# Two more projections in halves among a recurrence's steps, pooling sums as scans, and the last output tile in two pieces

## The chip, the cores and the metric

The kernel runs on one core of one Trainium2 chip. The metric is the device time of one execution in microseconds (us). Five engines work side by side, each through its own queue of instructions: TensorE (PE, whose weight loads appear as PEld), VectorE (DVE), ScalarE (ACT), GpSimd (POOL) and SyncE (SP, which starts most of the DMA transfers).

## The reference

One layer of a hybrid decoder trunk over 1024 tokens and 16 learned meta tokens (L = 1040) of width 1024, all in float32. Cut to what matters here:

```
u = rmsnorm(h);  q, f, i, g, v_pool, gate_a, gate_b = split(u @ w_in)
# recurrence, 4 heads of 128 keys and 128 values, state S:
f' = lb + (1 - lb) * sigmoid(f);   k = (1 - lb) * sigmoid(-f)
S[t] = f'[t] * S[t-1] + k[t] i[t]^T;   o[t] = q[t] S[t]
a = rmsnorm(o) * gain * sigmoid(g)
# pooling, 4 groups of 128 channels, windows w = 2, 4, 8, 16:
p = ((mean of the last min(w, t+1) rows of v_pool) - v_pool) @ pool_proj * scale
z = sigmoid(gate_a) * (a @ w_branch_hgrn) + sigmoid(gate_b) * (p @ w_branch_pool)
h = h + rmsnorm(z @ w_out)
u = rmsnorm(h);  y = gelu(causal_conv3(u @ w_gate) + bias) * (u @ w_up)
out = h + rmsnorm(y @ w_down)
```

## The kernel before

Nearly every matmul operand is kept as a high and a low part (`whi`/`wlo`, `uhi`/`ulo`, in a type with fewer mantissa bits that the PE takes faster), and a product is three matmuls: high by high, high by low, low by high. With the feature dimension on the partitions, a row of a projection is one matmul of 128 x 342 to 348 columns; 8 blocks of keys times 3 chunks of columns times 3 products make 72 rows for one projection.

The program runs in stages: norms, the gates `gate_a` and `gate_b` and the value projection of the recurrence (to about 265 us of the span), then **the heads' stage** (about 265 to 480 us), then the output projection and the feed-forward layer, whose products go through Strassen's scheme of seven products (to about 1090 us), and last the projection by `w_down`, whose end is the second place of the change.

**The heads' stage** is written by a table of words, `ORDER`. A word with a capital letter is a projection of one block of 128 output columns: `F`, `Q`, `G` (forget logit, query and output gate of the recurrence), `PV` (input of the pooling), `PP`, `BB`, `BA` (the products behind them), followed by the number of the head or group. `F3` is a whole projection; `Fa3` and `Fb3` are its two halves in time: `proj_parts` stops after half of its key blocks (rows L206, L207 and L210 of the profile) and goes on when the second word comes. The weights of each projection are cast on ACT (L152) and their low part taken on DVE, three blocks ahead, when the loader moves on. Between them, `h0` to `h3` take the next step of a head's recurrence (`head_steps`, a generator, one instance for each head):

- The score matrix of a head is put together from blocks on six levels (block lengths 2, 4, 8, 16, 32, 64). For each, DVE subtracts (L683), ACT takes two exponentials (L685, L686), DVE makes two products (L687, L688), all into a tile `d`, and PE multiplies it with itself into a bank `sl` (L698 for the levels from 32 up, L704 for the smaller). Levels go in pairs; a step issues DVE's and ACT's part of a pair ahead of PE's.
- Then come `kd`, the keys weighted by the decay to their chunk's end (L740 to L745), transposed on PE (L761 and L764) and copied (L762, L766); the products of the diagonal blocks (`sb`, L772); the chunk states `st` (L782 to L792, banks `ds`); the output `o` (L802 to L813, banks `po`); and the sums of its squares over the partitions (`ms`, L818 and L819), with a logarithm on ACT from each bank (L820) and one exponential (L821).

`c1` is the chain from a forget logit to its logarithm and running sum (`chain_f`, L629 to L636); ACT makes the sigmoids from the banks ahead of it (L624, L625). `sp0` and `sa0` split a pooled group or a head's output into high and low part, and `w0` to `w5` prepare weights of the feed-forward layer.

ACT changes its function table between sigmoids, exponentials, and the logarithms (an ACT_TABLE_LOAD row in the profile, at the line that needs it).

**Order.** Outside of blocks marked `manual_schedule`, the engines' orders are not those of the source: the framework's scheduler puts instructions into each engine's queue by a simulated timeline, with the order written as its start. Inside such a block the named engines follow the source. In both cases the resulting queues are fixed when the program is built, and an engine works through its own strictly in order. The tables of words thus set the order only in the large. Tiles of `slot` come from one pool of equal slots and `bank` is one of 8 PSUM banks, both handed on in turn; whoever takes one waits for the last reader of what was in it.

**Pooling.** `post_pv` copies the projection from its three banks to `vp` (ACT, L847) and forms the window sum by doubling on POOL (L854): one addition for w = 2, two for 4, three for 8, four for 16, ten in all, `cur[t] + cur[t - step]`. `pool_split` takes w times the mean minus the value on DVE.

**The end.** The last quarter of the `w_down` product, four tiles of 128 tokens by 512 columns, is summed in four banks `pd` over 22 key blocks: first the blocks from KT = 6 on for all four tiles, then the six that were prepared early (`held`), tile by tile. Behind each tile DVE subtracts (L1777), `half_norm` takes the sum of squares on ACT (L1701) and multiplies by the gain on DVE (L1702), and `finish` takes the root (ACT, L1708), its reciprocal (L1710), adds the residual for both halves of the row and stores them:

```
    for t in range(NT):
        for j in range(KT):
            multiply(banks, held[j], False, j == KT - 1, [t])
        dve.tensor_tensor(c11[t], banks[t], c11[t], ALU.subtract)
        half_norm(c11[t], t, 0)
        finish(t, c11[t], c12[t])
```

The functions that the change touches:

Of the kernel before, what the change touches and what calls it, by code (L numbers as in the profile page):

```python
# [42 lines left out]
KT = 6  # L43
# [11 lines left out]
ZA = 4  # L55
AHEAD = 3

ORDER = ("F0 c0 Q0 h0 F1 h0 h0 c1 Q1 h0 h1 h0 F2 h1 h1 c2 h0 h0 Qa2 Qb2 h1 h1 h2 G2 h0 h0 h1 Fa3 h1 h2 h0 h2 Fb3 "
# [3 lines left out]
POOLED = ()  # L62
# [7 lines left out]
def trunk_kernel(ctx: ExitStack, tc: tile.TileContext, x, meta_tokens, mix_norm_pre,  # L70
# [4 lines left out]
    act, dve, pool_e, pe = nc.scalar, nc.vector, nc.gpsimd, nc.tensor  # L75
# [43 lines left out]
    def small(shape, name, tag, bufs=4):  # L119
        return sm.tile(shape, F32, tag=tag, name=nm(name), bufs=bufs)  # L120
# [45 lines left out]
    class Loader:  # L166
# [10 lines left out]
        def next(self):  # L177
            self.at += 1
            return self.got[self.at - 1]
# [4 lines left out]
    def mm3(ps, a, b, first, last):  # L184
        (ahi, alo), (bhi, blo) = a, b
        pe.matmul(ps, ahi, bhi, start=first, stop=False)  # L186
        pe.matmul(ps, ahi, blo, start=False, stop=False)  # L187
        pe.matmul(ps, alo, bhi, start=False, stop=last)  # L188

    def proj(*a, **k):  # L190
        for banks in proj_parts(*a, **k):
            pass
        return banks
# [22 lines left out]
    class Strassen:  # L216
# [624 lines left out]

    def post_pv(g, pv):
        w = POOL_WINDOWS[g]
        vp, s1 = slot(L, name="vp"), slot(L, name="s1")
        s2 = slot(L, name="s2") if w > 2 else None
        for (lo, n), ps in zip(CH_ALL, pv):
            act.copy(vp[:, lo : lo + n], ps[:, :n])  # L847
        cur, step = vp, 1
        bufs = [s1, s2]
        while step < w:  # L850
            nxt = bufs[0]
            bufs = bufs[::-1]
            a = 2 * step - 1
            pool_e.tensor_tensor(nxt[:, a:L], cur[:, a:L], cur[:, a - step : L - step], ALU.add)  # L854
            cur, step = nxt, 2 * step
        pooled[g] = (cur, vp)

    def pool_split(g):
        w = POOL_WINDOWS[g]
        cur, vp = pooled[g]  # L860
        if w > T0 + 1:

            c1 = small([P, 1], "c1", "c1", 2)
# [128 lines left out]

    order = ORDER.split()
    order = [(o_[:-1], int(o_[-1])) for o_ in order]
# [57 lines left out]
    E = mybir.EngineType  # L1052
    with tc.manual_schedule(engines={E.Activation, E.DVE, E.PE}):
# [34 lines left out]
        for i in range(2, len(vtiles)):  # L1088
            ps = bank("pv")
# [80 lines left out]
    for kind, i in order:  # L1170
# [30 lines left out]
        if part == "a":  # L1201
# [3 lines left out]
        banks = proj(None, 0, n_k, xs, chunks, ws=ws, name="p" + kind.lower(),  # L1205
                     by_bank=2 if (kind, i) == ("BA", KD - 1) else 0)
# [307 lines left out]
    def next_rot():  # L1514
        rot[0] += 1
        return rot[0] % 2
# [138 lines left out]
    g4 = gain_bc(ffn_norm_post, "g4")  # L1655
    ssq4 = const.tile([P, 2, NCH], F32, name="ssq4")
    NT = NCH // 2

    def acc(i):
        return [big[0][:, 2 * i + t // 2, (t % 2) * 512 : (t % 2) * 512 + 512] for t in range(NT)]  # L1660

    u2, c21, c12, c11 = (acc(i) for i in range(4))
    c22 = u2

    def multiply(banks, ops, first, last, tiles=range(NT)):
        (yh, yl), (wh, wl) = ops
        for t in tiles:
            tt = slice(t * P, (t + 1) * P)
            mm3(banks[t], (yh[:, tt], yl[:, tt]), (wh, wl), first, last)

    def prep_last(k, hold):

        load_ops(3, k)
        if hold:
            hi, lo = slot(1024, F32R, "yh"), slot(1024, F32R, "yl")
        else:
            i = next_rot()
            hi, lo = big[1][:, i, :], big[1][:, 2 + i, :]
# [14 lines left out]
    junk = slot(512, name="junk4")  # L1693

    def load_h(t):
        hrow[t] = slot(D, name="hrow")
        nc.sync.dma_start(hrow[t], hs[HALO + t * P : HALO + (t + 1) * P, :])

    def half_norm(src, t, j):

        act.activation(junk, src, AF.Square, accum_out=ssq4[:, j, t : t + 1])  # L1701
        dve.tensor_tensor(src, src, g4[:, j * 512 : (j + 1) * 512], ALU.mult)  # L1702
        if j == 1:
            dve.tensor_scalar(ssq4[:, 1, t : t + 1], ssq4[:, 1, t : t + 1], 1.0 / D, EPS, ALU.mult, ALU.add)
# [27 lines left out]
    with tc.manual_schedule(engines={E.Activation, E.DVE}):  # L1732
        for s_ in range(3):
            banks = [[bank("pd") for _ in range(NT)] for _ in range(2)]
            for k in range(KH):
# [3 lines left out]
                if k == KH - 1:  # L1739
                    pa, pb = banks  # L1740
# [16 lines left out]


    banks = [bank("pd") for _ in range(NT)]
    for n, k in enumerate(range(KT, KH)):  # L1760
        if n == 0:
            prep_last(KH - 2, False)
            for t in range(NT):
                dve.tensor_tensor(c12[t], c12[t], pb[t], ALU.add)
            prep_last(KH - 1, False)
        multiply(banks, held.pop(k), n == 0, False)
        if n < NT:
            half_norm(c22[n], NT + n, 1)
            half_norm(c21[n], NT + n, 0)
            finish(NT + n, c21[n], c22[n])  # L1770
            load_h(n)
        if n > 0:
            half_norm(c12[n - 1], n - 1, 1)
    for t in range(NT):
        for j in range(KT):
            multiply(banks, held[j], False, j == KT - 1, [t])
        dve.tensor_tensor(c11[t], banks[t], c11[t], ALU.subtract)  # L1777
        half_norm(c11[t], t, 0)
        finish(t, c11[t], c12[t])
    close_pool("ps", "sm", "fm")  # L1780


# [27 lines left out]
```

## The time and the profile before

| | |
|---|---|
| time, median of 3 runs | 1324.69 us (1324.55 to 1325.63) |
| profiled execution | 1326.72 us, span 1325.0 us, mean granted PE clock 0.994 |
| PE | 1302.5 us busy, 98% of the span, 8665 matmuls |
| PEld | 1158.7 us, 87% |
| DVE | 948.7 us, 72% |
| ACT | 581.0 us, 44% |
| POOL | 355.5 us, 27% |
| heads' stage, 265 to 480 us | PE busy 204.0 of 215.0 us, DVE 153.6, ACT 145.1, POOL 24.1; granted clock 0.97 |

Shares of busy time are means over stages. The last row, from a table of busy time by stretches of the span, is for the stage that the change touches most: 11 us of PE's idle time lie in it. In the profile a row names the engine, the line, the operation, the tile written and those read, and in brackets what ended the engine's idle time ahead of it. A wait "PE sl L704 <- ACT ..." means that PE's row at L704 writing `sl` stood idle until that instruction was done.

### The profile page before, as it was taken

To read this page: it belongs to the slowest core of one execution; us is meant where nothing else is said; L and a number is where in the kernel's file an instruction comes from. 1 tells how busy PE (TensorE), PEld (TensorE's weight loads), DVE (VectorE), ACT (ScalarE), POOL (GpSimd) and SP (SyncE) were. 2 spreads that over 40 slices of the span, in tenths; PEclk is the share of its full clock that TensorE was granted. 3 is DMA by queue.
4 is the path that set the end of the run, shared out by engine and by line. 5 is a ranking of instruction groups with operands and counts; after the bars stand their busy time and mean duration, and the time that the engine had idled before them with its cause. 6 is when DMAs were issued, how large, how long until landed. Compare 5 with 4: busy or idle time off the path is not lost.

```text
span 1325.0 us, 21836 instructions
## 1 busy us (share of the span) xinstructions
PE 1302.5 (98%) x8665; PEld 1158.7 (87%) x8665; DVE 948.7 (72%) x1251; ACT 581.0 (44%) x978; POOL 355.5 (27%) x291
## 2 busy tenths in 40 slices
PE   8999999999899899999999999999999999999997
PEld 7799899999899899987898888888888888888886
DVE  6765545378768567775678999888998885455757
ACT  5553333368656755235564322222223233444443
POOL 3015422000011400061025555645646652000000
PEclk9999999999899999999999999999999999999999
DMA  8145433411110157987686777677767699666644
GB/s 273 42 107 160 125 106 103 127 50 49 36 52 20 46 180 263 353 284 253 234 281 234 179 212 191 187 206 176 175 162 168 150 258 305 212 223 222 222 175 159
DMA packets 139831, 230.55 MB, mean 174 GB/s; under 512 B 9080, under 2 KB 77340, under 8 KB 139730
## 3 DMA queue, kind: packets, MB, share of 16 engines
q1 hardware_dynamic: 127666, 204.78, 46.4%
q0 software_dynamic: 12064, 24.38, 11.2%
q8 instruction: 68, 1.11, 0.3%
q14 instruction: 33, 0.27, 0.1%
HBM read 165.59 MB, written 86.57 MB: 190 GB/s over the span
## 4 chain that ended last, share of the span: by engine, by line
PE 92%; DMA 3%; ACT 2%; DVE 1%; issue 1%; SPq 0%; DVEq 0%; ACTq 0%
PE P L309 15%; PE P L310 15%; PE P L312 15%; PE pd L186 5%; PE pd L187 5%; PE pd L188 5%; PE pm L186 2%; PE pm L187 2%; PE pm L188 2%; PE pf L206 1%; PE ppv L206 1%; PE pf L207 1%; PE ppv L210 1%; PE ppv L207 1%; PE pg L206 1%; PE pq L210 1%
## 5 line engine op out<-in xcount | busy, mean ns | idle before, releaser
L310 PE MATMUL P<-v,whi 128*128 128x512 f32 (+2 forms) x408 | 140.7, 353 | 0.0
L309 PE MATMUL P<-v,whi 128*128 128x512 f32 (+2 forms) x408 | 140.7, 352 | 0.0
L312 PE MATMUL P<-v,wlo 128*128 128x512 f32 (+2 forms) x424 | 135.1, 349 | 0.0
L1544 DVE TENSOR_TENSOR rot<-wraw,rot 128x1024 fp32r<-128x1024 f32 x31 | 38.0, 1224 | 72.2 <-ACT rot L1543 72.2
L309 PEld LDWEIGHTS P<-v,whi 128*128 128x128 f32 x408 | 76.7, 188 | 10.4
L310 PEld LDWEIGHTS P<-v,whi 128*128 128x128 f32 x408 | 76.6, 188 | 10.2
L254 ACT CAST whi<-wraw 128x512 fp32r<-128x512 f32 x78 | 46.1, 618 | 86.7 <-PE P L310 63.1
L312 PEld LDWEIGHTS P<-v,wlo 128*128 128x128 f32 x424 | 74.0, 188 | 10.8
L188 PE MATMUL pd<-rot 128*128 128x512 f32 x272 | 82.1, 389 | 0.0
L187 PE MATMUL pd<-rot 128*128 128x512 f32 x272 | 82.1, 389 | 0.0
L186 PE MATMUL pd<-rot 128*128 128x512 f32 x272 | 81.1, 389 | 0.1
L280 POOL TENSOR_TENSOR swa<-wraw,wraw 128x512 f32<-128x512 f32 x28 | 44.8, 1601 | 133.2 <-DMA wraw<-in_ffn_w_gate_dram 68.1
L1543 ACT CAST rot<-wraw 128x1024 fp32r<-128x1024 f32 x31 | 32.7, 1054 | 90.7 <-PE pd L188 89.4
L254 ACT CAST whi<-swa 128x512 fp32r<-128x512 f32 x56 | 33.4, 618 | 81.8 <-PE P L310 74.4
L255 DVE TENSOR_TENSOR wlo<-wraw,whi 128x512 fp32r<-128x512 f32 x74 | 65.6, 908 | 2.7 <-ACT whi L254 2.7
L255 DVE TENSOR_TENSOR wlo<-swb,whi 128x512 fp32r<-128x512 f32 x56 | 62.9, 1129 | 6.5 <-ACT whi L254 6.5
L1472 DVE SCALAR_TENSOR_TENSOR y<-g,par,y 128x1024 f32<-128x1024 f32 x44 | 64.3, 1461 | 0.8
L254 ACT CAST whi<-swb 128x512 fp32r<-128x512 f32 x56 | 33.4, 618 | 70.9 <-PE P L310 66.5
L186 PEld LDWEIGHTS pd<-rot 128*128 128x128 f32 x272 | 51.1, 188 | 11.1 <-DVE p L1480 0.5
L187 PEld LDWEIGHTS pd<-rot 128*128 128x128 f32 x272 | 51.0, 188 | 10.6
L188 PEld LDWEIGHTS pd<-rot 128*128 128x128 f32 x272 | 51.0, 188 | 10.6
L309 PE MATMUL P<-t4h,whi 128*128 128x258 f32 (+1 forms) x196 | 57.0, 307 | 0.0
(414 smaller groups left out, 4000.1 us busy)
## 6 DMA issues: line engine op xcount, KB each, us to landing
wraw<-in_w_in_dram SPq DMA_DIRECT2D x36, 512.0 KB, 4.9
yt<-ysum SPq DMA_DIRECT2D x33, 512.0 KB, 5.3
wraw<-in_ffn_w_gate_dram SPq DMA_DIRECT2D x26, 512.0 KB, 7.0
wraw<-in_ffn_w_up_dram SPq DMA_DIRECT2D x22, 512.0 KB, 4.6
wsum<-in_ffn_w_down_dram SPq DMA_DIRECT2D x22, 512.0 KB, 8.2
wraw<-in_w_out_dram SPq DMA_DIRECT2D x18, 512.0 KB, 4.3
ysum<-ys SPq DMA_DIRECT2D x11, 768.0 KB, 5.9
sa<-sscr SPq DMA_DIRECT2D x16, 513.0 KB, 6.5
```

The source lines that it names most:

```text
L186: pe.matmul(ps, ahi, bhi, start=first, stop=False)
L187: pe.matmul(ps, ahi, blo, start=False, stop=False)
L188: pe.matmul(ps, alo, bhi, start=False, stop=last)
L206: pe.matmul(ps[:, :n], whi[:, k, :], xhi, start=(k == 0), stop=False)
L254: act.copy(hi, src)
L255: (pool_e if 4 <= i < 2 * self.early else dve).tensor_tensor(lo, src, rr(hi), ALU.subtract)
L280: pool_e.tensor_tensor(s1, a21, a22, ALU.add)
L309: pe.matmul(d, whi[:, k, :], xh[:, c : c + w], start=(k == 0 and onto is None), stop=False, **go)
L310: pe.matmul(d, whi[:, k, :], xl[:, c : c + w], start=False, stop=False, **go)
L312: pe.matmul(x[:, o : o + w], wlo[:, k, :], xh[:, c : c + w], start=False, stop=(k == 3), **go)
L1472: dve.scalar_tensor_tensor(a, g[:, j : j + SEQ], cvw[:, j, m : m + 1], a, ALU.mult, ALU.add)
L1544: dve.tensor_tensor(lo, src, rr(hi), ALU.subtract)
```

## The change

**In the table of words:** `G2` is cut into `Ga2 h0 Gb2`, so that one more step of head 0 comes between its halves; a step of head 0 and one of head 2 that stood ahead of `Fb3` now follow it; and `PV1`, which stood whole behind the steps `h3 h2 h3 h1`, is cut in two, its first half ahead of those steps and its second half ahead of the `h1`. **In the pooling:** the doubling additions on POOL become one scan on DVE (new value in, value of w rows before out), or one addition for w = 2; 16 zeros ahead of `vp`, set by POOL, stand for what lies ahead of row 0; and the mean of row T0 = 14 for w = 16 is a scaled window sum instead of a sum of its own. **At the end:** the last tile is summed in two pieces of 256 columns in two banks (a fifth bank `pd`), and each is subtracted, squared and multiplied by the gain by itself, the gain product into a slot of its own (`left`); ACT and DVE follow the written order there; and of the additions into `c12`, the first goes ahead of the preparation of key block KH - 2.

```diff
-... Qa2 Qb2 h1 h1 h2 G2 h0 h0 h1 Fa3 h1 h2 h0 h2 Fb3 h2 c3 h2 PVa0 ...
+... Qa2 Qb2 h1 h1 h2 Ga2 h0 Gb2 h1 Fa3 h0 h1 h2 Fb3 h0 h2 h2 c3 h2 PVa0 ...
-... Q3 h1 h3 h0 h1 h2 h3 h2 h3 h1 PV1 h3 sp0 ...
+... Q3 h1 h3 h0 h1 h2 PVa1 h3 h2 h3 PVb1 h1 h3 sp0 ...
     def post_pv(g, pv):
         w = POOL_WINDOWS[g]
-        vp, s1 = slot(L, name="vp"), slot(L, name="s1")
-        s2 = slot(L, name="s2") if w > 2 else None
+        vz, cur = slot(NM + L, name="vp"), slot(L, name="s1")
+        vp = vz[:, NM:]
+        pool_e.memset(vz[:, :NM], 0.0)
         for (lo, n), ps in zip(CH_ALL, pv):
             act.copy(vp[:, lo : lo + n], ps[:, :n])
-        ...
-            pool_e.tensor_tensor(nxt[:, a:L], cur[:, a:L], cur[:, a - step : L - step], ALU.add)
-            cur, step = nxt, 2 * step
+        if w == 2:
+            dve.tensor_tensor(cur, vp, vz[:, NM - 1 : NM - 1 + L], ALU.add)
+        else:
+            dve.tensor_tensor_scan(cur, vp, vz[:, NM - w : NM - w + L], 0.0, ALU.add, ALU.subtract)
     def pool_split(g):
-            dve.tensor_reduce(c1, vp[:, 0 : T0 + 1], mybir.AxisListType.X, ALU.add)
-            dve.tensor_scalar(cur[:, T0 : T0 + 1], c1, float(w) / (T0 + 1), None, ALU.mult)
+            dve.tensor_scalar(cur[:, T0 : T0 + 1], cur[:, T0 : T0 + 1], float(w) / (T0 + 1), None, ALU.mult)
 ...
+    pieces = [(banks[-1], slice(0, 256)), (bank("pd"), slice(256, 512))]
+    def multiply_pieces(ops, first, last, which=pieces):
+        ...
+            mm3(ps[:, :256], (yh[:, tt], yl[:, tt]), (wh[:, n], wl[:, n]), first, last)
         if n == 0:
+            dve.tensor_tensor(c12[0], c12[0], pb[0], ALU.add)
             prep_last(KH - 2, False)
-            for t in range(NT):
+            for t in range(1, NT):
                 dve.tensor_tensor(c12[t], c12[t], pb[t], ALU.add)
-        multiply(banks, held.pop(k), n == 0, False)
+        ops = held.pop(k)
+        multiply(banks, ops, n == 0, False, range(NT - 1))
+        multiply_pieces(ops, n == 0, False)
 ...
+    with tc.manual_schedule(engines={E.Activation, E.DVE}):
+        for t in range(NT):
+            left = lefts[t % 2]
+            for i, (ps, n) in enumerate(pieces if t == NT - 1 else ((banks[t], slice(0, 512)),)):
+                ...
+                dve.tensor_tensor(c11[t][:, n], ps[:, : n.stop - n.start], c11[t][:, n], ALU.subtract)
+                part = t == NT - 1 and i == 0
+                act.activation(junk[:, n], c11[t][:, n], AF.Square, accum_out=sums4 if part else ssq4[:, 0, t : t + 1])
+                dve.tensor_tensor(left[:, n], c11[t][:, n], g4[:, n], ALU.mult)
+                if part:
+                    dve.scalar_tensor_tensor(ssq4[:, 1, t : t + 1], sums4, 1.0 / D, ssq4[:, 1, t : t + 1],
+                                             ALU.mult, ALU.add)
+            finish(t, left, c12[t])
```

Three places show what this does to the engines' queues. The number behind a name is the number of its buffer, which is not the same before and after. **Place A** is ACT's queue at the end of projection F3. Before, `d_3867` and `d_3873` are head 2's levels 8 and 16, `whi_3917` is the cast of the next weights, and `pf_3711` to `pf_3713` are the banks of F3:

```order
L783 COPY st_3813<-ds_3814 128x128
L685 ACTIVATE d_3867<-d_3867 128x64x8
L686 ACTIVATE d_3867<-d_3867 128x64x8
L685 ACTIVATE d_3873<-d_3873 128x32x16
L686 ACTIVATE d_3873<-d_3873 128x32x16
L152 CAST whi_3917<-wraw_3915 128x1024
L624 ACT_TABLE_LOAD
L624 ACTIVATE f_3923<-pf_3711 128x348
L625 ACTIVATE kk_3921<-pf_3711 128x348
```

In the same place after the change the same two levels are `d_3919` and `d_3925`, and F3's banks are `pf_3673` to `pf_3675`:

```order
L152 CAST whi_3851<-wraw_3849 128x1024
L624 ACT_TABLE_LOAD
L624 ACTIVATE f_3857<-pf_3673 128x348
L625 ACTIVATE kk_3855<-pf_3673 128x348
L624 ACTIVATE f_3857<-pf_3674 128x346
L625 ACTIVATE kk_3855<-pf_3674 128x346
L624 ACTIVATE f_3857<-pf_3675 128x346
L625 ACTIVATE kk_3855<-pf_3675 128x346
L783 COPY st_3865<-ds_3866 128x128
L685 ACT_TABLE_LOAD
L685 ACTIVATE d_3919<-d_3919 128x64x8
L686 ACTIVATE d_3919<-d_3919 128x64x8
```

The copy and the exponentials have moved from ahead of the cast to behind F3's sigmoids, with a table load ahead of them.

**Place B** is ACT's queue at head 1's sums of squares, where `d_4472` and `d_4478` are head 3's levels 8 and 16, `ms_4484` to `ms_4492` head 1's sums, and `vp_4580` takes PV1. Before:

```order
L685 ACTIVATE d_4472<-d_4472 128x64x8
L686 ACTIVATE d_4472<-d_4472 128x64x8
L820 ACT_TABLE_LOAD
L820 ACTIVATE rs_4325<-ms_4484,eps_t 128x342
L820 ACTIVATE rs_4325<-ms_4488,eps_t 128x342
L820 ACTIVATE rs_4325<-ms_4492,eps_t 128x342
L685 ACT_TABLE_LOAD
L685 ACTIVATE d_4478<-d_4478 128x32x16
L686 ACTIVATE d_4478<-d_4478 128x32x16
L821 ACTIVATE rs_4325<-rs_4325 128x1026
L152 CAST whi_4576<-wraw_4574 128x1024
L847 COPY vp_4580<-ppv_4499 128x348
```

After it, the levels are `d_4512` and `d_4518`, the sums `ms_4573` to `ms_4581`, and PV1 goes to `vp_4566`:

```order
L152 CAST whi_4562<-wraw_4560 128x1024
L820 ACT_TABLE_LOAD
L820 ACTIVATE rs_4326<-ms_4573,eps_t 128x342
L685 ACT_TABLE_LOAD
L685 ACTIVATE d_4512<-d_4512 128x64x8
L686 ACTIVATE d_4512<-d_4512 128x64x8
L820 ACT_TABLE_LOAD
L820 ACTIVATE rs_4326<-ms_4577,eps_t 128x342
L848 COPY vp_4566<-ppv_4376 128x348
L848 COPY vp_4566<-ppv_4377 128x346
L848 COPY vp_4566<-ppv_4378 128x346
L820 ACTIVATE rs_4326<-ms_4581,eps_t 128x342
```

The cast and the copies of `vp` come earlier, level 8's exponentials stand between the first and the second logarithm instead of ahead of them, and two more changes of table stand in the row (the fourth, ahead of `d_4518`, is the row behind the last one shown).

On PE the same place reads, before (`ppv_4499` to `ppv_4501` are the banks of PV1):

```order
L210 MATMUL ppv_4499<-uhi_88,wlo_3918 128x348
L210 MATMUL ppv_4500<-uhi_88,wlo_3918 128x346
L210 MATMUL ppv_4501<-uhi_88,wlo_3918 128x346
L704 MATMUL sl_4588<-d_4472 32x16 x32
L704 MATMUL sl_4627<-d_4478 32x16 x32
L206 MATMUL ppv_4677<-uhi_88,whi_4151 128x348
```

and after (`ppv_4376` to `ppv_4378` are the banks of PV1):

```order
L210 MATMUL ppv_4378<-uhi_88,wlo_3852 128x346
L818 MATMUL ms_4573<-rh_4353,onesr 128x342
L819 MATMUL ms_4573<-rl_4354,onesr 128x342
L818 MATMUL ms_4577<-rh_4353,onesr 128x342
L819 MATMUL ms_4577<-rl_4354,onesr 128x342
L818 MATMUL ms_4581<-rh_4353,onesr 128x342
L819 MATMUL ms_4581<-rl_4354,onesr 128x342
L704 MATMUL sl_4588<-d_4512 32x16 x32
L704 MATMUL sl_4627<-d_4518 32x16 x32
```

Head 1's `ms` sums, which stood ahead of most of PV1, have moved behind it, directly ahead of the two level products.

More of the change, by code (lines that the diff above doesn't have):

```diff
@@ L56 @@
 AHEAD = 3
-ORDER = ("F0 c0 Q0 h0 F1 h0 h0 c1 Q1 h0 h1 h0 F2 h1 h1 c2 h0 h0 Qa2 Qb2 h1 h1 h2 G2 h0 h0 h1 Fa3 h1 h2 h0 h2 Fb3 "
[1 row of a table removed]
+ORDER = ("F0 c0 Q0 h0 F1 h0 h0 c1 Q1 h0 h1 h0 F2 h1 h1 c2 h0 h0 Qa2 Qb2 h1 h1 h2 Ga2 h0 Gb2 h1 Fa3 h0 h1 h2 Fb3 "
[1 row of a table added]
          "sp1 PVb3 h2 h3 h3 sp3 PP1 h0 G3 h3 w0 PP2 PP3 w1 BB0 w4 h2 w4 BB1 BB2 BB4 w5 h3 BB3 w4 h3 w5 sa2 BB5 w5 "
@@ L843, in post_pv @@
         w = POOL_WINDOWS[g]
-        vp, s1 = slot(L, name="vp"), slot(L, name="s1")
-        s2 = slot(L, name="s2") if w > 2 else None
+        vz, cur = slot(NM + L, name="vp"), slot(L, name="s1")
+        vp = vz[:, NM:]
+        pool_e.memset(vz[:, :NM], 0.0)
         for (lo, n), ps in zip(CH_ALL, pv):
             act.copy(vp[:, lo : lo + n], ps[:, :n])
[L848 to L853, printed above, removed]
-            pool_e.tensor_tensor(nxt[:, a:L], cur[:, a:L], cur[:, a - step : L - step], ALU.add)
-            cur, step = nxt, 2 * step
+        if w == 2:
+            dve.tensor_tensor(cur, vp, vz[:, NM - 1 : NM - 1 + L], ALU.add)
+        else:
+            dve.tensor_tensor_scan(cur, vp, vz[:, NM - w : NM - w + L], 0.0, ALU.add, ALU.subtract)
         pooled[g] = (cur, vp)
@@ L861, in pool_split @@
         if w > T0 + 1:
-            c1 = small([P, 1], "c1", "c1", 2)
-            dve.tensor_reduce(c1, vp[:, 0 : T0 + 1], mybir.AxisListType.X, ALU.add)
-            dve.tensor_scalar(cur[:, T0 : T0 + 1], c1, float(w) / (T0 + 1), None, ALU.mult)
+            dve.tensor_scalar(cur[:, T0 : T0 + 1], cur[:, T0 : T0 + 1], float(w) / (T0 + 1), None, ALU.mult)
         dve.scalar_tensor_tensor(cur[:, T0:L], cur[:, T0:L], 1.0 / w, vp[:, T0:L], ALU.mult, ALU.subtract)
@@ L1759, in trunk_kernel @@
     banks = [bank("pd") for _ in range(NT)]
+    pieces = [(banks[-1], slice(0, 256)), (bank("pd"), slice(256, 512))]
+    def multiply_pieces(ops, first, last, which=pieces):
+        (yh, yl), (wh, wl) = ops
+        tt = slice((NT - 1) * P, NT * P)
+        for ps, n in which:
+            mm3(ps[:, :256], (yh[:, tt], yl[:, tt]), (wh[:, n], wl[:, n]), first, last)
     for n, k in enumerate(range(KT, KH)):
         if n == 0:
+            dve.tensor_tensor(c12[0], c12[0], pb[0], ALU.add)
             prep_last(KH - 2, False)
-            for t in range(NT):
+            for t in range(1, NT):
                 dve.tensor_tensor(c12[t], c12[t], pb[t], ALU.add)
             prep_last(KH - 1, False)
-        multiply(banks, held.pop(k), n == 0, False)
+        ops = held.pop(k)
+        multiply(banks, ops, n == 0, False, range(NT - 1))
+        multiply_pieces(ops, n == 0, False)
         if n < NT:
@@ L1773, in trunk_kernel @@
             half_norm(c12[n - 1], n - 1, 1)
[L1774 to L1779, printed above, removed]
+    lefts = [slot(512, name="left") for _ in range(2)]
+    sums4 = small([P, 1], "sums4", "mq", 6)
+    with tc.manual_schedule(engines={E.Activation, E.DVE}):
+        for t in range(NT):
+            left = lefts[t % 2]
+            for i, (ps, n) in enumerate(pieces if t == NT - 1 else ((banks[t], slice(0, 512)),)):
+                for j in range(KT):
+                    if t == NT - 1:
+                        multiply_pieces(held[j], False, j == KT - 1, pieces[i : i + 1])
+                    else:
+                        multiply(banks, held[j], False, j == KT - 1, [t])
+                dve.tensor_tensor(c11[t][:, n], ps[:, : n.stop - n.start], c11[t][:, n], ALU.subtract)
[6 more added lines that the diff above has]
+            finish(t, left, c12[t])
     close_pool("ps", "sm", "fm")
```

2 rows, old and new, of the table ORDER are left out of this document.

## The prediction

> **What bounds the kernel now.** I read the page's chain of waits first, then TensorE's (PE's) list of waits, then PE's busy time and clock in short windows.
>
> ```profile
> PE 92%; DMA 3%; ACT 2%; DVE 1%; issue 1%; SPq 0%; DVEq 0%; ACTq 0%
> PE pg L206 <- ACT rs L820: 3.4, 1, 3.4
> PE sl L704 <- issue: 2.7, 1, 2.7
> PE sb L772 <- DVE kk L754: 2.3, 1, 2.3
> PE sl L698 <- DVE near L719: 1.1, 1, 1.1
> PE ppv L206 <- ACT kk L625: 0.7, 1, 0.7
> ```
>
> PE is the bound nearly everywhere, so another engine's work costs something only where PE waits for it. The five waits below the first line lie among the heads' steps and sum to 10.2 us. Each long one is paid twice, as these windows of 3.41 us show (columns: PE busy, weight loads, DVE, ACT, POOL, granted clock, DMA share, GB/s):
>
> ```profile
> 335.02:338.44 3.42, 1.17 (x70) 0.91 (x68) 3.42 (x8) 3.37 (x7) 0.00 (x0) 1.00 0.52 152
> 338.44:341.85 3.41, 2.28 (x56) 2.08 (x43) 3.41 (x6) 3.40 (x6) 0.00 (x0) 0.50 0.02 5
> 341.85:345.27 3.42, 3.42 (x13) 3.42 (x13) 3.28 (x6) 3.35 (x8) 0.00 (x0) 0.50 0.07 19
> 399.88:403.29 3.41, 0.68 (x19) 0.64 (x19) 0.28 (x2) 2.59 (x4) 0.00 (x0) 1.00 0.03 10
> 403.29:406.71 3.42, 3.42 (x14) 3.42 (x13) 3.35 (x6) 2.18 (x3) 0.00 (x0) 0.50 0.02 5
> 457.90:461.31 3.41, 0.88 (x5) 0.88 (x6) 2.90 (x3) 3.38 (x7) 2.01 (x1) 1.00 0.00 0
> 461.31:464.73 3.42, 3.42 (x14) 3.42 (x13) 1.33 (x2) 3.39 (x5) 0.00 (x0) 0.50 0.52 156
> ```
>
> A window in which PE is busy for 0.68 to 2.28 of its 3.41 us is followed by one at half clock. PE works 2.28 + 3 x 3.42 = 12.5 us at half clock; at full clock that is about half the time, so some 6 us are lost. These stalls cost 10 + 6 = 16 us: that is the stake of the reordering, and it can be lost as well as won.
>
> **The change, part by part.** Times are those of the profiled execution: 1326.7 us with a span of 1325.0; the median of the three runs is 2.0 us lower.
>
> *G2 in halves.* Head 0's transposes of `kd` (L761) now follow G2's first half. Here are the first matmul of the second half before, and the product of `kd` for which the transposes wait:
>
> ```profile
> 328.86 0.32 PE L206 MATMUL pg<-uhi,whi 128*128 128x342 f32 x1
> 329.70 1.23 DVE L745 TENSOR_TENSOR kd<-kd,kk 128x1040 f32<-128x1040 f32 x1
> ```
>
> PE comes to the transposes at 328.86 and waits until 330.93: 2.1 us. In return the waits of 2.3 and 1.1 us go: the block product L772 now stands behind 36 more rows of G2 and half of F3, and its operand on DVE is done by then. Net -1.3 in idle time; one half-clock window in place of two.
>
> *Place A, behind F3.* Before, ACT made head 2's exponentials of levels 8 and 16 (L685, L686, buffers 3867 and 3873) before F3 ended, and 30 rows of F3 still covered DVE's products. Now the same exponentials (3919, 3925) stand on ACT behind the cast that waits for F3's end, a table load, F3's six sigmoids, a copy and another table load. The prices:
>
> ```profile
> 353.45 0.63 ACT L685 ACTIVATE d<-d 128x512 f32<-128x512 f32 x1
> 353.99 0.61 ACT L686 ACTIVATE d<-d 128x512 f32<-128x512 f32 x1
> 354.14 0.68 DVE L688 TENSOR_TENSOR d<-d,kk 128x512 f32<-128x512 f32 x1
> 358.94 1.05 ACT L152 CAST whi<-wraw 128x1024 fp32r<-128x1024 f32 x1 [4.34 <-PE pf L207]
> 360.01 1.28 ACT L624 ACT_TABLE_LOAD   x1
> 361.30 0.46 ACT L624 ACTIVATE f<-pf 128x348 f32<-128x348 f32 x1
> 363.01 0.51 ACT L625 ACTIVATE kk<-pf 128x346 f32<-128x346 f32 x1
> 387.14 0.29 ACT L783 COPY st<-ds 128x128 f32<-128x128 f32 x1
> 350.55 0.48 PE L782 MATMUL ds<-vmeta,ktm 16*128 16x128 f32 x2
> 352.54 0.41 PE L206 MATMUL pf<-uhi,whi 128*128 128x348 f32 x1
> 359.31 1.33 PE L704 MATMUL sl<-d 128*32 128x16 f32 x128
> ```
>
> From the cast's start to the last sigmoid's end: 363.52 - 358.94 = 4.58. Copy 0.29, table load 1.28, the pair of exponentials 1.15 (353.45 to 354.60), DVE's product 0.68: together 8.0 us before PE may do level 8. In that time PE has F3's last three rows (0.5), the `ds` matmuls (350.55 to 352.54: 2.0) and half of what row 359.31 shows (0.7): 3.2 us. Idle: at least 4.8. ACT may also be late at the cast: it had 4.34 us to spare, but now has two more table loads ahead (the sigmoids of G2 are cut apart by exponentials) and copies that wait for DVE, so between 0 and 2.6 late; I take 1.4, about the middle: 6.2. Level 16 waits 0.6 more (another pair of exponentials, less PE's 0.6 on level 8), and the 0.7 at `ppv` goes. The next block product, for head 1, stands behind a DVE queue set back by this: 0 up to the 2.3 of its like above; I take 0.8. Net +6.9.
>
> *Place B, PV1 in halves.* The step between the halves takes away the 2.7 us wait, since a half of PV1 stands ahead of it. But before, 48 rows of PV1 stood between head 1's `ms` sums and levels 8 and 16 of head 3; now all of PV1 is done before the sums, nothing follows, and on ACT the logarithms L820 are cut apart by the exponentials, with a table load at each change:
>
> ```profile
> 408.80 0.64 PE L819 MATMUL ms<-rl,onesr 128*128 128x342 f32 x3
> 409.53 1.42 ACT L820 ACTIVATE rs<-ms,eps_t 128x342 f32<-128x342 f32 x3
> 410.97 1.28 ACT L685 ACT_TABLE_LOAD   x1
> 377.77 1.14 ACT L847 COPY vp<-ppv 128x348 f32<-128x348 f32 x3
> ```
>
> First wait: behind PV1's last matmuls ACT has a cast 1.05, table load 1.28, one logarithm 0.5, table load 1.28, exponentials 1.15, then DVE 0.68: 6.0 us. PE has 3 rows of PV1 and 6 of `ms` at 0.16: 1.4. Idle 4.6. Second wait, counted from the end of those exponentials: table load 1.28, logarithm 0.44, three copies of `vp` 1.05, logarithm 0.44, table load 1.28, exponentials 1.15, DVE 0.68 = 6.3, against PE's 0.7 wait for the first product and 0.6 to 1.25 (half clock) on level 8: idle 4.4 to 5.0, I take 4.6. Net +9.2 - 2.7 = +6.5.
>
> *G3's wait of 3.4* goes down: its first bank is freed by a copy of the transposes (L762) instead of by L820 behind its table load. Between 0 and 3.4 remains; I take 1.6: -1.8.
>
> *Pooling on DVE.* Ten POOL additions become three scans and one addition on DVE, whose price is known from the same kind and length:
>
> ```profile
> L636 DVE TENSOR_TENSOR_SCAN b<-keep_on,f 128x1040 f32<-128x1040 f32 x4 | 9.3, 2325 | 0.2
> ```
>
> That is 3 x 2.3 + 1.2 = 8.2 us on DVE, queued ahead of head products. At A and B ACT comes last, not DVE, and POOL's sums released none of the five waits: I take 0, with 0 to 2.3 (one scan ahead of a product) for the range. The small memsets on POOL stand well ahead of their readers. SP's queue keeps its order.
>
> *The end.* The rows that carry it:
>
> ```profile
> 109.00 0.28 PE L309 MATMUL P<-uhi,whi 128*128 128x256 f32 x1
> 109.12 0.28 PE L310 MATMUL P<-ulo,whi 128*128 128x256 f32 x1
> 1317.38 0.39 PE L187 MATMUL pd<-yl,yh 128*128 128x512 f32 x1
> 1317.61 0.39 PE L188 MATMUL pd<-yh,yl 128*128 128x512 f32 x1
> 1318.04 0.69 DVE L1777 TENSOR_TENSOR acc<-pd,acc 128x512 f32<-128x512 f32 x1 [0.38 <-PE pd L188]
> 1318.76 0.63 ACT L1701 ACTIVATE junk<-acc 128x512 f32<-128x512 f32 x1 [3.03 <-DVE acc L1777]
> 1319.52 0.29 ACT L1708 ACTIVATE std<-ssq 128x1 f32<-128x1 f32 x1
> 1319.52 0.69 DVE L1702 TENSOR_TENSOR acc<-acc,g 128x512 f32<-128x512 f32 x1 [0.79 <-ACT junk L1701]
> 1320.12 0.16 DVE L1710 RECIPROCAL rstd<-std 128x1 f32<-128x1 f32 x1
> ```
>
> Half-width matmuls start 0.12 apart, full ones 0.23: 33 matmuls of the last tile become 66, +0.3 us. After the last matmul the subtraction and the square run on half the columns: they lose nearly 0.5 (the 1040-column product above took 1.23 against 0.68 for 512, so 256 take about 0.4). The gain product is off the chain, so the reciprocal follows the root: 0.25. Net -0.4. The bank that the extra piece needs is freed by the `c12[0]` addition, now first; 9 matmuls of PE cover it, and at worst PE waits that row's 0.7.
>
> **Sum.** Idle: -1.3 + 6.9 + 6.5 - 1.8 = +10.3. Half clock: 12.5 us of work before; now about one window behind the transposes, one and a half behind A, two behind and between B's waits, perhaps one behind G3: some 16 us, +1.5 (from -2 to +4). End -0.4. Together +11.4: 1326.7 + 11.4 = 1338.1 in a profiled execution, 2.0 less in the median: 1336.1.
>
> The Trainium skill, "TensorE: Matmul & The Clock Gate", Part 1, lets the clock fall to half after an idle window of about 3.4 us. The windows here fell after 0.68 to 2.28 us of work, so the trace differs; if only a fully idle window counted, some 5 us of my half-clock time would go and the sum would be about 1331.
>
> **Rivals.** (1) *Faster:* the halves feed PE where it starved, A and B hide, and all old waits go: 16 us and 0.4 won, 1308. It decides at ACT's queue: the exponentials would have to be ready before PE has done the 3.2 us at A and 1.4 us at B. For it: the two waits cut by the halves do go. Against it: 8.0 and 6.0 us of ACT and DVE rows in strict sequence. 0.04. (2) *The idle time only moves:* ACT is early at A (4.8), `vp`'s copies and logarithms hide B's second wait, head 1's product and G3 wait for nothing: 2.1 + 4.8 + 4.6 = 11.5 against 10.2, two half windows fewer, end -0.4: 1322 to 1327. Against it: B's second wait has two table loads of its own. 0.05. (3) *Every table switch costs more than its row:* ACT drains too, 1.4 us at each of six loads in A's and B's chains, 1344. Against it: 360.01 + 1.28 ends where 361.30 starts. 0.03. The Trainium skill, "ScalarE: Activation LUTs", What ACT_TABLE_LOAD costs, puts such a drain at 1.38 us beside 1.28 for the load; only the load is in the trace. (4) *The windows fall badly and a scan stands ahead of a product:* +4 and +3, 1343. 0.08. My forecast, 1329 to 1341: 0.80.
>
> **Numbers.** A measurement of this kernel tells 0.2% (2.6 us) from no change. Faster 0.05 (rival 1 and a piece of 2), same 0.05, slower 0.90. The range from 1328.5 to 1344 leaves out rivals 1 and 2 and a tail.
>
> **What would show it.** Right: PE waits at `sl` L704 for `d` L687/L688 three times, one near 6 and two of 4 to 5 us, half-clock windows behind each, 36 table loads instead of 31, no wait of 2.7 at the step inside PV1, and an end shorter by half a microsecond. Wrong: PE busy through F3's end and PV1's end; or a long wait whose releaser is a scan.

## The result and the profile after

The changed kernel takes 1333.93 us in the median (1333.54 to 1335.19, 4 runs), the kernel before 1324.62 us (1321.42 to 1325.63, 4 runs). The ratio is 1.0076, 95% interval 1.0058 to 1.0094: slower by 0.76%. The forecast was 1336.1 us, 1328.5 to 1344. The profiled execution took 1333.88 us with a span of 1332.2, that is 7.2 us more than the profiled one of before. (That one was slower than its kernel's median by 2 us, the profiled one of the changed kernel was not; so the profiles lie closer together than the medians.)

Where the 7.2 us lie is seen first in two stretches of the same work, from the first row of F0 to the first row of the first `BB` product. The first row is before, the second after (columns: PE busy, PE's weight loads, DVE, ACT, POOL, granted clock, DMA share, GB/s):

```profile
268.73:478.46 209.73, 198.73 (x2605) 191.34 (x2603) 148.42 (x212) 142.27 (x244) 24.11 (x14) 0.97 0.15 43
```
```profile
268.56:486.70 218.14, 197.53 (x2605) 189.85 (x2603) 152.10 (x215) 149.01 (x249) 3.16 (x8) 0.96 0.14 41
```

The heads' stage alone grew by 8.4 us. PE does the same 2605 matmuls and is busy for 1.2 us less, so all of it, and a little more, is idle time. PE's waits in this stage, after the change:

```profile
PE sl L704 <- DVE d L688: 16.3, 4, 5.9
PE pt L761 <- DVE kd L745: 2.0, 1, 2.0
PE pg L206 <- ACT kt L762: 1.3, 1, 1.3
```

Five waits of 10.2 us have become six of 19.6 (a wait of 0.6 to 0.7 us at `pq`, the same before and after, is left out of both). Four stand at the small levels' products, one pair at place A (the end of F3) and one at place B (head 1's sums). Here they are in the timeline of PE, with the wait ahead of each row in brackets:

```profile
361.42 1.05 PE L704 MATMUL sl<-d 128*32 128x16 f32 x64 [5.88 <-DVE d L688]
363.24 1.05 PE L704 MATMUL sl<-d 128*32 128x16 f32 x64 [0.76 <-DVE d L688]
...
421.89 1.05 PE L704 MATMUL sl<-d 128*32 128x16 f32 x64 [4.83 <-DVE d L688]
...
427.79 1.05 PE L704 MATMUL sl<-d 128*32 128x16 f32 x64 [4.85 <-DVE d L688]
```

And the sequence on ACT and DVE that PE waits for at place A, from the cast of the next weights to level 8's last product:

```profile
353.36 1.05 ACT L152 CAST whi<-wraw 128x1024 fp32r<-128x1024 f32 x1
354.43 1.28 ACT L624 ACT_TABLE_LOAD   x1
...
357.44 0.50 ACT L625 ACTIVATE kk<-pf 128x346 f32<-128x346 f32 x1
357.78 0.32 ACT L783 COPY st<-ds 128x128 f32<-128x128 f32 x1
358.12 1.28 ACT L685 ACT_TABLE_LOAD   x1
359.41 0.63 ACT L685 ACTIVATE d<-d 128x512 f32<-128x512 f32 x1
359.95 0.61 ACT L686 ACTIVATE d<-d 128x512 f32<-128x512 f32 x1
360.68 0.69 DVE L688 TENSOR_TENSOR d<-d,kk 128x512 f32<-128x512 f32 x1
```

From 353.36 to 361.37 nothing stands still on ACT and DVE together: 8.0 us, row by row what the prediction added up. The clock around the two places, in windows of 3.41 us:

```profile
356.61:360.03 3.42, 0.00 (x0) 0.00 (x0) 1.71 (x4) 3.39 (x8) 0.00 (x0) 1.00 0.52 154
360.03:363.44 3.41, 1.26 (x80) 1.15 (x84) 3.37 (x7) 3.39 (x6) 0.00 (x0) 0.50 0.00 1
363.44:366.86 3.42, 3.42 (x73) 3.38 (x66) 2.59 (x7) 2.54 (x3) 0.11 (x1) 0.50 0.02 5
418.06:421.47 3.41, 0.00 (x0) 0.00 (x0) 1.97 (x3) 3.36 (x5) 0.00 (x0) 1.00 0.07 19
421.47:424.88 3.41, 1.05 (x64) 0.95 (x64) 1.23 (x2) 3.38 (x7) 0.00 (x0) 0.50 0.02 5
424.88:428.30 3.42, 0.51 (x38) 0.54 (x42) 3.41 (x4) 3.41 (x5) 0.00 (x0) 0.50 0.00 0
428.30:431.71 3.41, 3.41 (x52) 3.37 (x45) 3.41 (x6) 0.42 (x1) 0.00 (x0) 0.50 0.00 0
```

Five windows at half clock instead of four, but in three of them PE stands idle for most of the time: 1.26 + 3.42 + 1.05 + 0.51 + 3.41 = 9.7 us of work at half clock, where it was 12.5 before. No other window of the stage is at half clock, neither behind the 2.0 at the transposes nor behind G3's 1.3.

The end: the first matmul of the last section in both kernels, then the last matmul and the reciprocal that stands on the chain to the last store, after the change (those of before are in the prediction).

```profile
1287.92 0.39 PE L186 MATMUL pd<-yh 128*128 128x512 f32 x1
```
```profile
1295.28 0.39 PE L186 MATMUL pd<-yh 128*128 128x512 f32 x1
...
1325.55 0.28 PE L188 MATMUL pd<-yh,yl 128*128 128x256 f32 x1
...
1327.28 0.16 DVE L1704 RECIPROCAL rstd<-std 128x1 f32<-128x1 f32 x1 [0.44 <-ACT std L1702]
```

From the section's first matmul to its last it is now 30.27 us, and was 29.69: +0.58. From the last matmul to the reciprocal it is 1.73, and was 2.51: -0.78.

### The profile page after: what moved, and what is told of

It reads as the page before. It is cut to its first block, busy times and chain, and to the rows that moved or that the text cites. A ratio compares the mean times of both kernels' runs of the same rounds, so it can differ in the third digit from the quotient of the medians.

```text
span 1332.2 us, 21907 instructions
## 1 busy us (share of the span) xinstructions
PE 1300.0 (98%) x8698; PEld 1158.0 (87%) x8698; DVE 956.6 (72%) x1257; ACT 588.1 (44%) x985; POOL 335.4 (25%) x285
## 4 chain that ended last, share of the span: by engine, by line
PE 92%; ACT 4%; DVE 2%; DMA 2%; issue 1%; SPq 0%; DVEq 0%; ACTq 0%
PE P L309 15%; PE P L310 15%; PE P L312 15%; PE pd L186 5%; PE pd L187 5%; PE pd L188 5%; PE pm L186 2%; PE pm L188 2%; PE pm L187 2%; PE pf L206 1%; PE pbb L206 1%; PE pbb L207 1%; PE pf L207 1%; PE pbb L210 1%; PE ppv L206 1%; PE pv L187 1%
## 5 line engine op out<-in xcount | busy, mean ns | idle before, releaser
L310 PEld LDWEIGHTS P<-v,whi 128*128 128x128 f32 x408 | 76.6, 188 | 10.2
```

The costliest lines, as they stand in the source:

```text
L310: pe.matmul(d, whi[:, k, :], xl[:, c : c + w], start=False, stop=False, **go)
```

## The experiments

The times below are ratios to the kernel before, measured on the same chip.

**e1: the end alone.** The part of the change from `banks = ...` on, with ORDER and pooling of before.

```diff
+    pieces = [(banks[-1], slice(0, 256)), (bank("pd"), slice(256, 512))]
...
+    with tc.manual_schedule(engines={E.Activation, E.DVE}):
```

> The kernel before with the change at the end alone (last tile in two pieces, the c12[0] addition first, ACT and DVE in written order); ORDER and pooling as before. My theory: -0.4 us (66 half-width matmuls cost 0.3 more than 33, and behind the last one 0.7 to 0.8 goes), so within 1 us of before; PE's waits among the heads' steps the same to 0.1 us. Rival: the written order on ACT and DVE makes the norms of the first tiles late and PE waits for the bank of the extra piece, +1 us or more.

Ratio 0.9999, interval 0.9989 to 1.0010: nothing that can be told from zero (-1.5 to +1.3 us). The times alone would not exclude the rival's microsecond, but PE has no wait in the last projection of this trace, and among the heads' steps it has the waits of before to 0.1 us.

**e2: place B alone.**

```diff
-... h2 h3 h2 h3 h1 PV1 h3 sp0 ...
+... h2 PVa1 h3 h2 h3 PVb1 h1 h3 sp0 ...
```

> The kernel before with PV1 alone in halves (place B); G2, F3, pooling and end as before. My theory: B's price is made by the order of ACT's queue, so it comes without the scans: the wait of 2.7 us at the step goes, two waits of 4.6 to 5.0 us at sl L704 for d L688 come, half-clock windows around them; +6.5 to +8 us, and G3's wait stays near 3.4 us if it hangs on the pooling, or falls to 1.3 us if it hangs on this part of the order. Rival (the scans on DVE make the loss): no wait over 3 us here and a time within 2 us of before.

Ratio 1.0069 (1.0057 to 1.0081), +9.1 us. Without any scan on DVE the two waits are there, so the order makes them; the rival falls. G3's wait stayed at 3.3 us, so this part of the order does not take it away. But the cost is above the range, and the second wait is 6.26 us where the whole change has 4.85. The timeline of this kernel at that place shows why:

```profile
419.47 1.92 POOL L854 TENSOR_TENSOR s<-s 128x1037 f32<-128x1037 f32 x1
...
419.82 2.12 DVE L687 TENSOR_TENSOR d<-d,q 128x512 f32<-128x512 f32 x1 [4.51 <-ACT d L685]
...
422.68 1.06 PE L704 MATMUL sl<-d 128*32 128x16 f32 x64 [6.26 <-DVE d L688]
```

DVE's product takes 2.12 us here, and 0.69 in the changed kernel; the difference of 1.43 is that of the two waits (1.41). A POOL addition runs beside it. Run e8 tests that.

**e3: place A and G2 alone.**

```diff
-... h2 G2 h0 h0 h1 Fa3 h1 h2 h0 h2 Fb3 h2 c3 h2 PVa0 ...
+... h2 Ga2 h0 Gb2 h1 Fa3 h0 h1 h2 Fb3 h0 h2 h2 c3 h2 PVa0 ...
```

> The kernel before with G2 in halves and the steps around F3 as in the changed kernel (place A); PV1, pooling and end as before. My theory: the waits of 2.3 and 1.1 us give way to one of 2.0 at the transposes; a wait of 5.9 and one of 0.8 us come at sl L704; the half-clock windows move from 338-345 us to those behind the 5.9; the 2.7 us wait at the step inside PV1 and G3's 3.4 us stay: +4 to +6 us. Rival (the scans make the loss): within 2 us of before. The sum of this run's and e2's difference should come to about 2 us above the whole change's, because the pooling and the end give something back.

Ratio 1.0032 (1.0021 to 1.0043), +4.2 us, inside the range. PE's waits are those expected, with 5.86 and 0.76 at place A:

```profile
PE sl L704 <- DVE d L688: 6.6, 2, 5.9
PE pg L206 <- ACT rs L820: 3.4, 1, 3.4
PE sl L704 <- issue: 2.5, 1, 2.5
PE pt L761 <- DVE kd L745: 2.0, 1, 2.0
```

G3's 3.4 is untouched here too. The two parts of the order together cost 13.3 us, about 4 more than the whole change and not the expected 2: pooling and end must give back more than I thought.

**e4: the old order with the new pooling and the new end.** The changed kernel with the table of words of before.

> The changed kernel with the table of words of before: pooling as scans on DVE and the new end, nothing else. My prediction's terms (pooling 0, end -0.4) give -0.4 us; if the fall of G3's wait (3.4 to 1.3 us) belongs to the pooling and not to the order, it appears here and the time is 2 to 4 us under before, with the half-clock window behind it gone. Rival (the 8.2 us of scans on DVE stand ahead of head products): +2 to +4 us, with a wait whose releaser is a scan or a product queued behind one.

Ratio 0.9969 (0.9958 to 0.9981), -4.1 us: faster than the kernel before, just beyond the range of 2 to 4. Since the end alone is worth nothing measurable (e1), this is the pooling. In this kernel's waits G3's is the one that changed:

```profile
PE sl L704 <- issue: 2.8, 1, 2.8
PE sb L772 <- DVE kk L754: 2.2, 1, 2.2
PE pg L206 <- ACT kt L762: 1.3, 1, 1.3
```

With other instructions on POOL and DVE the scheduler has put the two copies of the transposes (`kt`) ahead of the logarithms in ACT's queue, as its timeline shows:

```profile
456.52 1.07 ACT L762 COPY kt<-pt 128x512 f32<-128x512 f32 x2
...
458.56 1.28 ACT L820 ACT_TABLE_LOAD   x1
```

G3 now waits for a copy, where it waited for the first logarithm behind its table load. The half-clock window behind G3 is gone with it. So the fall of G3's wait, which I had counted, belongs to the pooling and not to the order of words.

**e5: one word moved back, place A.**

```diff
-... Ga2 h0 Gb2 h1 Fa3 h0 h1 h2 Fb3 h0 h2 h2 c3 h2 ...
+... Ga2 h0 Gb2 h1 Fa3 h0 h1 h2 h2 Fb3 h0 h2 c3 h2 ...
```

> The changed kernel with one word moved: the step of head 2 that issues levels 8 and 16 stands ahead of Fb3 again (Fa3 h0 h1 h2 h2 Fb3 h0 h2 c3); both halves, pooling and end stay. On ACT the four exponentials then stand ahead of the weight cast and the sigmoids. My theory (A's price is the place of the step, not the halves): the waits of 5.9 and 0.8 us at place A shrink to 2 to 3 us in all, the half-clock windows behind them to none or one, B's 4.8 and 4.9 and the 2.0 at the transposes stay: 5 to 7 us faster than the changed kernel, that is 1327 to 1329 us. Rival (halving itself sets DVE and PE back): within 2 us of the changed kernel, with the wait at another row.

Ratio 1.0035 (1.0023 to 1.0047), median 1328.65: 5.4 us under the changed kernel (0.41% of 1325), in the range. Place A now costs 0.4 and 0.6 us of waits instead of 6.6 (2 to 3 were expected), with both halves in place. B's waits are 4.83 and 4.84, unchanged. So at A it is the place of the step, and not the cut, that costs.

**e6: no change of table at place B.**

```diff
-            act.activation(rs[:, lo : lo + n], ps[:, :n], AF.Ln, bias=eps_t)
+            act.activation(rs[:, lo : lo + n], ps[:, :n], AF.Square if h == 1 else AF.Ln, bias=eps_t)
```

> The changed kernel with head 1's three logarithms behind the sums of squares computed as squares, which need no other function table; the output is another, every queue's order the same but for four table loads of 1.28 us at place B. My theory (strict sequence on ACT, each load costs its row): the first wait falls from 4.8 to 2.3 if only ACT sets it, or to 3.3, since DVE's subtraction for level 16 (417.88 to 419.10 in the changed kernel's trace) then comes last; the second falls from 4.9 to 2.3, or 2.6 if the scan of 2.3 us stands ahead of the product; about 4 us less idle, 3 to 6 us faster with the half-clock windows. Rival (a change of table costs about twice its row): both waits under 1 us, 8 us or more faster. Rival (DVE's scans set the waits): first and second wait as before, within 1 us of the changed kernel.

Ratio 1.0039 (1.0025 to 1.0052), median 1330.56: 4.9 us under the changed kernel (0.37%). The two waits at B:

```profile
421.98 0.74 PE L704 MATMUL sl<-d 128*32 128x16 f32 x64 [3.31 <-DVE d L688]
...
425.49 1.06 PE L704 MATMUL sl<-d 128*32 128x16 f32 x64 [2.78 <-DVE d L688]
```

The first fell by 1.52 and not by two loads (2.56): DVE's subtraction for level 16 came last, as the second of the two cases said. The second fell by 2.07; it had two loads less, but now the scan of 2.32 us stood ahead of level 16's product. The rival with twice the price per load would have left under 1 us of each; it falls. Loads cost their row here.

**e7: another order.** The changed kernel's pooling and end; in the table, among smaller moves, G2 and PV1 are whole, head 2's steps stand ahead of Fb3, and head 1's sums (`h1`) stand two words behind PV1.

```diff
-... Q1 h0 h1 h0 F2 ... h1 h1 h2 Ga2 h0 Gb2 h1 Fa3 h0 h1 h2 Fb3 h0 h2 h2 c3 h2 ...
+... Q1 h1 h0 h0 F2 ... h1 h1 G2 h0 h0 h1 h2 Fa3 h1 h0 h2 h2 h2 Fb3 c3 h2 ...
-... Q3 h1 h3 h0 h1 h2 PVa1 h3 h2 h3 PVb1 h1 h3 sp0 h3 sa1 PV2 h2 h2 PP0 h3 PVa3 h3 sp2 h2 sp1 PVb3 h2 h3 h3 sp3 PP1 ...
+... Q3 h1 h2 h3 h0 h1 h3 h2 h3 PV1 sp0 h3 h1 h3 PV2 h2 sa1 h3 PP0 h2 PVa3 h3 sp2 h2 sp1 PVb3 h3 sp3 h3 h2 PP1 ...
```

> The changed kernel's pooling and end with another table of words: G2, PV1 whole, head 2's steps for levels 8 and 16 ahead of Fb3, head 1's sums of squares behind PV1 and one step of head 3, and a few steps of heads 1 and 3 moved by a place. By my theory the waits are a matter of what covers each step: none over 1.5 us is left from 265 us on (before: 3.4, 2.7, 2.3, 1.1), no half-clock window, so against the run with the old order (1320.7 us, waits of 2.8, 2.2, 1.3 and 1.2 us and two stretches at half clock with some 7 us of work) 9 to 11 us less: 1310 to 1312 us. Rival (idle time only moves): the waits turn up at other rows and the time is within 3 us of 1320.7.

Ratio 0.9885 (0.9870 to 0.9900), median 1310.22: 15 us faster than before and 25 faster than the changed kernel (differences of the ratios times 1325), in the range. The longest of PE's waits from 265 us on are these two:

```profile
PE pba L206 <- ACT whi L162: 1.1, 1, 1.1
PE pq L206 <- ACT kk L625: 0.7, 1, 0.7
```

No window of the stage is at half clock, and the mean granted clock is 0.999. The stake that the prediction named (16 us) can nearly be won, with the operations of the changed kernel. Several words moved at once here; which of the moves brings how much was not separated.

**e8: two additions on POOL beside the scan.**

```diff
             dve.tensor_tensor_scan(cur, vp, vz[:, NM - w : NM - w + L], 0.0, ALU.add, ALU.subtract)
+            if g == 1:
+                s2 = slot(L, name="s2")
+                pool_e.tensor_tensor(s2, vp, vp, ALU.add)
+                pool_e.tensor_tensor(s2, vp, vp, ALU.add)
```

> The changed kernel with two additions on POOL more for group 1 (vp + vp of 1040 columns into a tile that nobody reads), as long as the two that the old pooling did there; the scan on DVE stays, PE's queue is the same, DVE's and ACT's up to level 16's products. In e2's trace the product L687 for level 16 took 2.12 instead of 0.69 us while a POOL addition of 1.92 us ran beside it. Theory (an addition on POOL and a DVE instruction with two inputs keep each other out): the additions start when vp is copied, at about 423.9 us, and end at about 427.8 or later; the scan or the product L687 takes 1.4 us or more longer than its own 2.3 or 0.69, and the second wait at B grows from 4.85 to 6.3 to 9 us; time 1.5 to 5 us above the changed kernel. Rival (the 2.12 of e2 was a matter of something else, such as a late operand): scan 2.3, product 0.69, second wait 4.8 to 4.9, the same time as the changed kernel.

Ratio 1.0117 (1.0095 to 1.0139), 5.4 us above the changed kernel (0.41%), a little over the range. In the timeline:

```profile
424.15 1.92 POOL L855 TENSOR_TENSOR s<-vp 128x1040 f32<-128x1040 f32 x1 [6.77 <-ACT vp L848]
424.16 4.09 DVE L852 TENSOR_TENSOR_SCAN s<-vp 128x1040 f32<-128x1040 f32 x1 [2.17 <-issue]
...
426.15 3.81 POOL L856 TENSOR_TENSOR s<-vp 128x1040 f32<-128x1040 f32 x1
...
428.17 2.34 DVE L687 TENSOR_TENSOR d<-d,q 128x512 f32<-128x512 f32 x1
...
431.26 1.06 PE L704 MATMUL sl<-d 128*32 128x16 f32 x64 [8.23 <-DVE d L688]
```

The engines take turns: the scan (2.32 alone) ends 2.2 us after the first addition, the second addition (1.92 alone) ends 1.7 us after the scan, and the product (0.69 alone) half a microsecond after that. The wait grew from 4.85 to 8.23, in the upper part of the range. The rival (something else in e2) falls.

## Why the prediction was right, and where it was not

**The stage and the sign: right.** The forecast case came: idle time of one queue moved behind another's, +9.4 us of waits (19.6 against 10.2) where the sum had +10.3. Of the signs that it named, the long waits at `sl`, the missing 2.7 us wait and the 36 table loads (31 before) came; the end is shorter by 0.2 us and not by half a microsecond.

**G2 in halves: right,** 2.05 for 2.25 and 1.13: -1.3.

**Place A: right in its mechanism, a little too large.** Forecast 6.2 and 0.6, measured 5.88 and 0.76. The cast came 1.1 us after F3's last L207 row had ended (351.90 + 0.32), for which I had taken 1.4. The 0.8 us for head 1's block product did not come; the 0.7 at `ppv` went. Net +5.9 against +6.9. e5 shows the reason to be the place of one step.

**Place B: right.** 4.83 and 4.85 less 2.73: +6.95 against +6.5. e2 shows that the order alone makes it, e6 that ACT's table loads carry a part and that DVE stands close behind ACT, which the prediction had not seen in the first chain: it had counted ACT alone ahead of the product. In the second chain the scan and ACT tie in the changed kernel's trace: the scan ends at 426.34 (424.01 + 2.33), the exponential that level 16's product needs at 426.32 (425.69 + 0.63), and the product starts at 426.35. So "At A and B ACT comes last, not DVE" holds there with nothing to spare.

**G3: right in size (-2.1 against -1.8) and in what releases it (a copy, L762), silent on which part of the change does it.** It comes with the pooling (e4), and the order of words leaves it as it was (e2, e3).

**Half clock: the term with the wrong sign.** Forecast +1.5 us for 16 us of work, measured -1.4 for 9.7. The failed step read two kinds of windows as one: "A window in which PE is busy for 0.68 to 2.28 of its 3.41 us is followed by one at half clock". The 2.28 belonged to a window that was at half clock already. Of the windows at full clock only those up to 1.40 fell; so the waits of 2.0 and 1.3 us, for which I had counted a window each, cost none in this execution. Besides, PE stood idle in much of the windows behind A and B, so that they hold less work than I took. The last section has the rows.

**Pooling on DVE: a term of nothing that was not nothing.** "POOL's sums released none of the five waits: I take 0, with 0 to 2.3". Pooling and end are worth -4.1 us (e4), the end none of it that can be measured (e1). Part of that is G3's fall, which the sum had as a term of its own without saying that the pooling makes it. The rest is mostly clock. Here is e4's row for the same stretch as in the section on the result:

```profile
268.58:473.57 204.99, 196.01 (x2604) 188.63 (x2603) 152.40 (x215) 142.43 (x244) 3.15 (x8) 0.98 0.15 44
```

It is 4.7 us shorter than before. PE's waits are 1.9 us less, and at half clock PE works 6.5 us (3.41 + 3.07) instead of 12.5, which is 3.0 less; together 4.9. Of the 3.0, 1.7 is the window behind G3. Most of the rest is the second window at 338 to 345 us, which is missing here behind the same two waits: where the windows fell in this execution, and no merit of the pooling.

I had also asked only whom POOL's sums release, and not what runs more slowly beside them. Here is the subtraction for the levels on DVE, before and after (shortest, median and longest of 24, in ns):

```profile
L683 DVE TENSOR_TENSOR d<-b x24: 1200/1218/2932, 269.4 to 424.6; 128x1024 f32<-128x1024 f32 x24
```
```profile
L683 DVE TENSOR_TENSOR d<-b x24: 1198/1218/1248, 269.3 to 433.7; 128x1024 f32<-128x1024 f32 x24
```

The longest stands beside a POOL addition, and with the additions gone no subtraction takes over 1.25 us. In the kernel before it costs nothing that the trace shows, since none of PE's waits hangs on it. With the new order a row lengthened in this way (the product L687) does stand ahead of a wait: the second wait at B is 6.26 us with the additions on POOL (e2) and 4.85 without them.

**The end: right in its parts, smaller in sum.** The tail behind the last matmul gave 0.78 for the forecast 0.75. From the section's first matmul to its last it is 0.58 more and not 0.3. The starts, for which I had taken 0.12 and 0.23, are 0.120 and 0.227 apart when measured over many rows, and 66 of the one are 0.4 more than 33 of the other; 0.1 more comes in because the last matmul, now half as wide, starts that much nearer to the end. Net -0.2 against -0.4; in time it can't be told from nothing. (The sum runs over 11 key blocks, 33 matmuls a tile; the 22 in the description of the kernel is a slip.)

The trace has 7.2 us where the sum had 11.4: 0.9 too much idle time and 2.9 too much half clock make 3.8, 0.2 too much gain at the end goes the other way, and 0.6 is left: the stages that the sum left out are 1.0 shorter, and the heads' stage is 0.4 longer than its waits and its clock make it. The median moved by 9.3 us, and e2, e3 and e4 together come to +9.2, each known to about 1.5. So the mechanism was right, and the forecast of 1336.1 came within 2.2 us of the median although its half-clock term had the wrong sign; that the term was small is luck in part, since it hangs on where the windows fall.

## What to carry to other kernels

Cutting a projection to fill a wait moves other steps' work behind its end; before it is done, walk the queue of the engine that prepares the next operands, with its table loads, from the cut's last release to the matmul that needs them, and set against it what the matmul engine still has. Work that waits for nothing and releases nobody can still cost, when it makes the rows beside it longer: compare the longest row of a kind with its median, and look whether a wait hangs on it. And where waits are the loss, the place of a single step can decide: one word was worth 5.4 us with all cuts in place (e5), and the fastest order here has G2 and PV1 whole (e7).

## What the runs showed of the hardware

**The clock falls and rises at two different shares of work.** In the nine profiles with half-clock windows in this stage (all but e7's), windows of 3.41 us at full clock with PE busy for 1.40 us or less (21 windows) were followed by one at half clock, and those with 1.48 or more never. Out of half clock, windows up to 2.78 us stayed there, and those from 3.07 on were followed by full clock. The four rows next to the edges, with the row that follows each, are from e6 (1.40, falls), e2 (1.48, stays), e1 (2.78, stays at half) and e4 (3.07, rises):

```profile
327.79:331.20 3.41, 1.40 (x10) 1.15 (x9) 3.41 (x4) 3.41 (x7) 0.00 (x0) 1.00 0.00 0
331.20:334.62 3.42, 3.42 (x16) 3.34 (x15) 3.42 (x7) 2.38 (x6) 0.00 (x0) 0.50 0.00 0
```
```profile
334.08:337.49 3.41, 1.48 (x13) 1.17 (x11) 3.41 (x6) 3.32 (x5) 0.00 (x0) 1.00 0.54 154
337.49:340.90 3.41, 1.91 (x99) 1.79 (x100) 3.41 (x9) 3.38 (x6) 0.00 (x0) 1.00 0.02 5
```
```profile
339.17:342.58 3.41, 2.78 (x38) 2.72 (x39) 3.38 (x8) 3.39 (x8) 0.00 (x0) 0.50 0.07 19
342.58:346.00 3.42, 3.42 (x14) 3.42 (x13) 3.28 (x4) 2.92 (x6) 0.32 (x1) 0.50 0.00 0
```
```profile
401.25:404.66 3.41, 3.07 (x25) 3.04 (x26) 2.59 (x5) 1.24 (x3) 0.00 (x0) 0.50 0.03 5
404.66:408.07 3.41, 3.41 (x23) 3.41 (x23) 3.33 (x5) 3.08 (x5) 0.00 (x0) 1.00 0.00 0
```

So a single wait costs a window if about 2.0 us of it (3.41 - 1.40) fall into one. By this a wait of 4 us does so wherever the windows lie, and one of 2.0 only by chance: the wait at the transposes was 2.0 to 2.1 us in the changed kernel, e3, e5, e6 and e8, and cost a window in e3 and e6 alone. The Trainium skill, "TensorE: Matmul & The Clock Gate", Part 1, asks for an idle window to fall and a busy one to rise; the runs here have a window 41% busy that falls and one 90% busy that suffices to rise.

**An addition on POOL and a two-input instruction on DVE exclude each other.** Scan 4.09 for 2.32 us, product 2.12 and 2.34 for 0.69, addition 3.81 for 1.92 (e2, e8). The Trainium skill, "SBUF — State Buffer", Who interferes with whom, says that an instruction of DVE with two inputs in SBUF and one of GpSimd that reads SBUF take turns on a shared port, the loser waiting for the whole instruction; the rows here agree, and show it for the scan too.
